# One norm for all tokens, the logits' products beside it, and a moved set of values in an attention layer's opening

## The chip, the cores and the metric

The kernel runs on one core of a Trainium2 chip. The metric is the device time of one launch in microseconds (us). Engines are named as in the profile: PE is TensorE's matmul row and PEld its weight loads, DVE is VectorE, ACT is ScalarE, POOL is GpSimd, SP is SyncE, which here issues DMAs. TensorE's clock has two levels in the records, 1.2 and 2.4 GHz, shown as a granted clock of 0.50 and 1.00.

## The reference, cut to what matters

Two layers over 1024 prompt tokens and 32 sample tokens (1056 columns in all, width 1024). Layer 0 is a gated convolution and a feed-forward block. Layer 1 is attention with a forget bias, then another feed-forward block.

```
kvf = rmsnorm(x, kv_norm) @ w_kv                 # keys, values, one forget logit per head
logf = log_sigmoid(kvf[..., 2 * D_ATT:] + b_f)
c = cumsum(concat(cached logf, logf))            # over tokens, per head
q = rmsnorm(x, b_norm) @ w_q
s = q @ k.T * HEAD_DIM ** -0.5 + c[query] - c[key]
o = softmax(where(key <= query, s, -inf)) @ v    # 16 heads of 64
x = x + o @ w_o
```

## The kernel before

Activations lie transposed: features on the 128 partitions, the 1056 tokens along the free axis. Weights and activations are split into a high and a low part, and each product of a 128x128 weight block is three matmuls (lines 259 to 261, `chain`). A unit of weights (128 output features) over all tokens is 72 such matmuls, in three chunks of tokens (384, 384 and 288 columns) of 8 steps.

A root-mean-square norm is one factor per token, and it is applied to the products rather than to x. `start` notes the sum of squares `acc`. The first units of a stage are multiplied out without it (`outer`), kept raw, and `settle` (line 296) then makes the factor and multiplies the raw tiles. `rstd` (line 313) makes it in three thirds of 352 tokens: `rstd_steps` (line 323) sums over partitions with one-column matmuls (line 334), takes a root on ScalarE (line 336), makes a Newton step on VectorE (lines 338 to 342), lays the factors on a diagonal `dg` (line 344), spreads them over all partitions with a matmul against ones (line 348) and copies them out (line 349). The mixer (layer 0) uses this for its first two units, the attention layer for its first.

The attention layer opens in `attention` (line 1259). `first` (line 1335) yields the values of the first pair of heads, then the keys and queries of head 0, step by step. `forget` (line 889) makes the logits and their running sums, and the two generators run in turns. `forget` multiplies the logits' weights by x (lines 913, 914), norms z (line 917), turns it (line 922), takes log-sigmoid on ScalarE and VectorE (lines 925 to 938), loads the cached logits into `frun` (line 943), sums over tokens with a triangle matmul (lines 950, 951), splits the sums into high and low parts (`ch`, `ekt`, `eqt`, lines 959 to 968), turns them (line 978), copies them out of PSUM (line 985) and writes them to DRAM (line 986). `rows` (line 1028) reads four rows per head back into partitions 64 to 67 of that head's operands `kb` and `qb`, which the second matmul of the scores uses (line 1092).

Then `weave` runs the attention of 16 heads as the main work and hangs filler steps between: `fillers(h)` (line 1326) gives head h the keys of head h + 1 (12 steps) and the values of the next pair (8 steps beside an even head, 4 beside an odd one). The last head's filler is the output product.

The order on each engine is not that of the code. The framework puts all instructions into queues before the run, by priority (earlier code first, raised by `high_priority` for attention's own work) and by its own estimates of time. On the chip each engine's queue is then in order. PSUM has six tiles in this phase: three named d, two s (two banks each) and one o. Of the 24 SBUF tiles of the pool "x", 16 hold the split activations here; the logits' tiles and the heads' operands share the others.

Of the kernel before, what the change touches and what calls it, by code (L numbers as in the profile page):

```python
# [18 lines left out]
D = 1024  # L19
SEQ = 1024  # L20
# [66 lines left out]
class Net:  # L87
# [187 lines left out]
    def unit(self, src, xs, dst, before=0):  # L275


        nc = self.nc
        h, l = self.ready.pop(0) if self.ready else self.weights(src)
        w = [(h[:, k], l[:, k]) for k in range(NK)]  # L280
        if self.fresh:
            for t, c in zip(self.outer(w, xs, CH), CH):
                for p, d in spread(c, before):
                    nc.scalar.activation(dst[:, d], t[:, p.start - c[0]:p.stop - c[0]], AF.Copy)
            self.raws.append((dst, before))
            self.fresh -= 1
            if not self.fresh:
                self.settle()
            return
        for c in CH:  # L290
            ps = self.dbank()[:, :c[1] - c[0]]
            self.chain(ps, w, xs, c)
            for p, d in spread(c, before):
                nc.vector.tensor_mul(dst[:, d], ps[:, p.start - c[0]:p.stop - c[0]], self.rs[:, p])

    def settle(self):

        for r, c in self.rstd(self.acc):
            for t, before in self.raws:
                for p, d in spread(c, before):  # L300
                    self.nc.vector.tensor_mul(t[:, d], t[:, d], r[:, p.start - c[0]:p.stop - c[0]])
# [8 lines left out]
        nc.scalar.activation(sq, x, AF.Square)  # L310
        return lambda: (nc.vector if hurry or m == NK - 1 else nc.gpsimd).tensor_add(acc, acc, sq)

    def rstd(self, acc, cuts=CH):

        out = self.rs = self.slot("rstd", None, F32, *self.rtag)
        for c in cuts:
            for _ in self.rstd_steps(acc, out, c):
                pass  # L320
            yield out[:, slice(*c)], c

    def rstd_steps(self, acc, out, c, own=False):

        nc = self.nc
        cs, n = slice(*c), (c[1] - c[0]) // SIDE

        def bank():
            return self.bank(self.spare()) if own else self.dbank()

        ps = bank()[:SIDE, :n]
        for i in range(n):
            a = c[0] + i * SIDE
            nc.tensor.matmul(ps[:, i:i + 1], acc[:, a:a + SIDE], self.ones[:, :1], start=True, stop=True)
        e, w, r = (self.sm.tile([SIDE, n], F32, name="n" + k, tag="n" + k, bufs=2) for k in "ewr")
        nc.scalar.activation(e, ps, AF.Sqrt, bias=self.epst[:SIDE], scale=1.0 / D)
        yield
        nc.vector.tensor_scalar(w, ps, -0.5 / D, -0.5 * EPS, op0=OP.mult, op1=OP.add)
        nc.vector.reciprocal(r, e)
        nc.vector.tensor_mul(e, r, r)  # L340
        nc.vector.tensor_mul(e, e, w)
        nc.vector.scalar_tensor_tensor(r, e, 1.5, r, op0=OP.add, op1=OP.mult)
        dg = self.diag([SIDE, n, SIDE])
        nc.vector.tensor_mul(dg, self.ident[:SIDE, None, :SIDE].to_broadcast([SIDE, n, SIDE]),
                             r[:, :, None].to_broadcast([SIDE, n, SIDE]))
        yield
        ps = bank()[:, :c[1] - c[0]]
        nc.tensor.matmul(ps, self.ones[:SIDE], dg.rearrange("p n c -> p (n c)"), start=True, stop=True)
        nc.scalar.activation(out[:, cs], ps, AF.Copy)
        yield  # L350
# [538 lines left out]
    def forget(self, xs):  # L889
# [14 lines left out]
        nc.vector.tensor_add(tri, tri, self.ident)  # L904
        f, u, v, d, e, lf, base, c = (self.keep("f" + n, [128, nb, H]) for n in "zuvdelbc")
        nc.vector.memset(f, 0.0)
        z = self.keep("z", [H, TT])
        low = self.keep("zl", [H, TT])
        for t in CH:
            n = t[1] - t[0]  # L910
            ps = self.bank("s")
            for k, (xh, xl) in enumerate(xs):
                nc.tensor.matmul(ps[:48, :n], w[:, k], xh[:, t[0]:t[1]], start=(k == 0), stop=False)
                nc.tensor.matmul(ps[:48, :n], w[:, k], xl[:, t[0]:t[1]], start=False, stop=(k == NK - 1))
            nc.scalar.activation(low[:, t[0]:t[1]], ps[32:32 + H, :n], AF.Copy)
            nc.vector.tensor_add(z[:, t[0]:t[1]], ps[:H, :n], low[:, t[0]:t[1]])
            nc.vector.tensor_mul(z[:, t[0]:t[1]], z[:, t[0]:t[1]], self.rs[:H, t[0]:t[1]])
        yield
        ps = self.bank("s")[:, :nb * H].rearrange("p (b h) -> p b h", h=H)
        for b in range(NK + 1):  # L920
# [17 lines left out]
        nc.vector.scalar_tensor_tensor(lf, f, 0.0, v, op0=OP.min, op1=OP.subtract)  # L938
        nc.sync.dma_start(a["o_f"][:SEQ].rearrange("(b p) h -> p b h", p=128), lf[:, :NK])
        nc.sync.dma_start(a["o_f"][SEQ:], lf[:ls, NK])  # L940
        run = self.keep("frun", [128, nb, H])
        nc.vector.memset(run, 0.0)
        nc.sync.dma_start(run[:, NK + 1], a["c_f"])
        nc.vector.tensor_copy(run[:, :NK], lf[:, :NK])
        nc.vector.tensor_copy(run[:ls, NK], lf[:ls, NK])
        for _ in range(3):
# [21 lines left out]
        nc.vector.tensor_sub(eq[:, :, :, 3], c, chf)  # L968
        yield
        yield  # L970
        for src, dst, old in ((ek, self.kb, self.cb), (eq, self.qb, None)):
            t = self.keep("er", [4 * H, TT])
            for b0 in range(0, NK + 1, 4):
                ps = self.bank("s")
                n = min(512, TT - b0 * 128)
                for b in range(b0, min(NK + 1, b0 + 4)):
                    m = min(128, TT - b * 128)
                    nc.tensor.transpose(ps[:4 * H, (b - b0) * 128:(b - b0) * 128 + m],
                                        src[:m, b].rearrange("p h r -> p (h r)"), self.ident[:m, :m])
                if b0 + 4 > NK and old is not None:  # L980
                    nc.tensor.transpose(ps[:4 * H, 128:256], src[:, NK + 1].rearrange("p h r -> p (h r)"), self.ident)
                    told = self.keep("er2", [4 * H, PAST])
                    nc.scalar.activation(told, ps[:4 * H, 128:256], AF.Copy)
                    nc.sync.dma_start(old, told)
                nc.scalar.activation(t[:, b0 * 128:b0 * 128 + n], ps[:4 * H, :n], AF.Copy)
            nc.sync.dma_start(dst, t)

    def scratch(self):

# [269 lines left out]
    def attention(self, x, parts, after):  # L1259
# [5 lines left out]
        self.heads, self.vs = [], {}  # L1265
        forget = self.forget(xs)

        def dense(src, gain, put):


            h, l = self.weights(src, gain)
            w = [(h[:, t], l[:, t]) for t in range(NK)]
            if self.fresh:
                raw = self.temp("raw")
                for t, c in zip(self.outer(w, xs, CA), CA):
                    nc.scalar.activation(raw[:, c[0]:c[1]], t, AF.Copy)
                self.raws.append((raw, 0))
                self.fresh = 0
                self.settle()
                for c in CA:  # L1280
                    put(raw[:, c[0]:c[1]], c)
                yield
                return
            for c in CA:
                d, n = self.dbank()[:, :c[1] - c[0]], c[1] - c[0]
                for k in range(NK):
                    self.chain(d, w, xs, c, range(k, k + 1))
                    if k % 2 and k + 1 < NK:
                        yield
                t = self.slot("stage", [128, 384], F32, "stage", 3)  # L1290
                nc.vector.tensor_mul(t[:, :n], d, self.rs[:, c[0]:c[1]])
                put(t[:, :n], c)
                yield

        def keys(h):
# [5 lines left out]
        def values(p):  # L1301
            vp = self.vs[p] = self.slot("vp", [128, NK + 1, 256], F32R, "vp", 2)
            yield from dense(a["w_v"][p], (self.gain[:, 2],), lambda t, c: self.values(p, vp, t, c))

        def outs():

# [19 lines left out]
        def fillers(h):  # L1326
            if h == HEADS - 1:
                return 3 * NK, outs()
            p = h // 2 + 1
            if p < NP and h % 2 == 0:  # L1330
                half[p] = values(p)
            n = (4 if h % 2 else 8) if p < NP else 0
            return 12 + n, mixed(h + 1, half.get(p), n)

        def first():
            yield from values(0)
            yield from keys(0)

        for _ in zip_longest(first(), forget):
            pass  # L1340
        self.rows(self.heads[0])
        self.weave(self.attend(), 13.0, fillers)
        self.wide = True
        ws = self.resident(a["w_o"][4:])
# [133 lines left out]
```

## Time and profile before

| what | value |
|---|---|
| median of 3 runs | 2549.89 us (2549.51 to 2549.95) |
| profiled execution | 2550.09 us |
| its span, first to last instruction | 2548.3 us |
| mean granted TensorE clock | 0.989 |
| PE busy | 2471.9 us, 97% of the span, 18484 matmuls |
| DVE, ACT, POOL busy | 1531.6, 1216.5 and 899.3 us |

The time of a launch is a little longer than the span of its instructions. A busy PE is not PE at its peak, since matmuls are pipelined and the clock can be granted at half; an idle engine other than the bounding one costs nothing. In a timeline row the brackets give how long the engine stood idle before it and what ended that wait.

### The profile page before, as it was taken

To read this page: it belongs to the slowest core of one execution; us is meant where nothing else is said; L and a number is where in the kernel's file an instruction comes from. 1 tells how busy PE (TensorE), PEld (TensorE's weight loads), DVE (VectorE), ACT (ScalarE), POOL (GpSimd) and SP (SyncE) were. 2 spreads that over 40 slices of the span, in tenths; PEclk is the share of its full clock that TensorE was granted. 3 is DMA by queue.
4 is the path that set the end of the run, shared out by engine and by line. 5 is a ranking of instruction groups with operands and counts; after the bars stand their busy time and mean duration, and the time that the engine had idled before them with its cause. 6 is when DMAs were issued, how large, how long until landed. Compare 5 with 4: busy or idle time off the path is not lost. (4 is left out here: it accounts for less than half of the span.)

```text
span 2548.3 us, 47227 instructions
## 1 busy us (share of the span) xinstructions
PE 2471.9 (97%) x18484; PEld 2433.1 (95%) x18484; DVE 1531.6 (60%) x2617; ACT 1216.5 (48%) x2388; POOL 899.3 (35%) x952
## 2 busy tenths in 40 slices
PE   7999999999999999998999999999999999999996
PEld 6999999999999999997999999999999999999996
DVE  5434438855555555665677677665875555555575
ACT  4111114555555555444566666653454555555454
POOL 3000012344444444342455444422244444443423
PEclk9999999999999999998999999999999999999998
DMA  3111123376766666631233222373247676666752
GB/s 111 45 48 50 42 77 98 70 120 120 122 119 114 116 118 119 139 113 50 75 80 80 77 76 71 80 251 104 72 88 125 116 121 119 111 117 116 122 141 69
DMA packets 147631, 254.76 MB, mean 100 GB/s; under 512 B 22352, under 2 KB 58320, under 8 KB 147408
## 3 DMA queue, kind: packets, MB, share of 16 engines
q0 software_dynamic: 41472, 77.88, 23.0%
q1 hardware_dynamic: 105936, 173.87, 22.7%
q8 instruction: 145, 2.38, 0.4%
q14 instruction: 78, 0.64, 0.1%
HBM read 130.52 MB, written 113.04 MB: 96 GB/s over the span
## 5 line engine op out<-in xcount | busy, mean ns | idle before, releaser
L711 PE MATMUL pb_p<-b,wb 128*128 128x264 f32 x6720 | 894.9, 284 | 1.8 <-ACT u L753 1.8
L711 PEld LDWEIGHTS pb_p<-b,wb 128*128 128x128 f32 x6720 | 850.0, 188 | 2.2 <-ACT u L753 2.2
L877 POOL DMA_DIRECT2D xd<-xs x288 | 262.1, 914 | 494.9 <-ACT xs L875 493.6
L875 ACT ACTIVATE xs<-pb_d 128x264 f32<-128x264 f32 x576 | 218.3, 387 | 349.4 <-PE pb_d L261 309.8
L259 PE MATMUL pb_d<-acth,wb 128*128 128x264 f32 x1152 | 327.8, 285 | 1.6 <-ACT xs L875 1.6
L260 PE MATMUL pb_d<-actl,wb 128*128 128x264 f32 x1152 | 327.5, 285 | 0.0
L261 PE MATMUL pb_d<-acth,wb 128*128 128x264 f32 x1152 | 327.3, 285 | 0.0
L259 PE MATMUL pb_d<-xh,wh 128*128 128x384 f32 (+2 forms) x864 | 285.3, 333 | 8.4 <-ACT xh L248 7.6
L260 PE MATMUL pb_d<-xl,wh 128*128 128x384 f32 (+2 forms) x864 | 285.2, 330 | 5.6 <-DVE xl L249 5.5
L261 PE MATMUL pb_d<-xh,wl 128*128 128x384 f32 (+2 forms) x864 | 283.6, 328 | 0.0
L478 DVE SCALAR_TENSOR_TENSOR y<-u,cv,y 128x1058 f32<-128x1058 f32 x186 | 238.8, 1329 | 54.9 <-ACT y L474 54.8
L259 PEld LDWEIGHTS pb_d<-acth,wb 128*128 128x128 f32 x1152 | 216.6, 188 | 2.8 <-ACT xs L875 2.5
L261 PEld LDWEIGHTS pb_d<-acth,wb 128*128 128x128 f32 x1152 | 216.8, 188 | 0.0
L260 PEld LDWEIGHTS pb_d<-actl,wb 128*128 128x128 f32 x1152 | 216.8, 188 | 0.0
L236 ACT ACTIVATE wh<-wraw 128x1024 fp32r<-128x1024 f32 (+1 forms) x69 | 72.3, 1047 | 259.6 <-PE pb_o L260 125.3
L460 POOL COPY u<-cv 128x4 f32<-128x4 f32 x96 | 63.5, 662 | 355.7 <-DVE u L668 256.9
L701 DVE TENSOR_TENSOR wb<-wr,wb 128x512 fp32r<-128x512 f32 x196 | 154.2, 788 | 56.0 <-ACT wb L700 44.7
L701 DVE TENSOR_TENSOR wb<-ws,wb 128x512 fp32r<-128x512 f32 x160 | 126.1, 789 | 98.6 <-ACT wb L700 98.6
L259 PEld LDWEIGHTS pb_d<-xh,wh 128*128 128x128 f32 x864 | 164.7, 191 | 9.8 <-ACT xh L248 8.0
L260 PEld LDWEIGHTS pb_d<-xl,wh 128*128 128x128 f32 x864 | 165.1, 191 | 7.9 <-DVE xl L249 7.4
L733 POOL TENSOR_TENSOR ws<-wr 128x512 f32<-128x512 f32 x80 | 121.7, 1521 | 134.9 <-DMA wr<-in_w_up 120.8
L261 PEld LDWEIGHTS pb_d<-xh,wl 128*128 128x128 f32 x864 | 164.8, 191 | 0.3
(347 smaller groups left out, 4964.2 us busy)
## 6 DMA issues: line engine op xcount, KB each, us to landing
xd<-xs POOLq DMA_DIRECT2D x288, 264.0 KB, 4.3
wr<-in_w_up SPq DMA_DIRECT2D x168, 256.0 KB
wr<-in_w_down SPq DMA_DIRECT2D x80, 256.0 KB
x<-xd SPq DMA_DIRECT2D x48, 264.0 KB
wraw<-in_w_in SPq DMA_DIRECT2D x23, 512.0 KB
xd<-x SPq DMA_DIRECT2D x64, 132.0 KB
wraw<-in_w_kq SPq DMA_DIRECT2D x16, 512.0 KB
xd<-x SPq DMA_DIRECT2D x16, 264.0 KB
```

The source lines that it names most:

```text
L236: nc.scalar.activation(h[:, i:j], raw[:, i:j], AF.Copy)
L259: nc.tensor.matmul(ps, wh, xh[:, c[0]:c[1]], start=(i == 0), stop=False)
L260: nc.tensor.matmul(ps, wh, xl[:, c[0]:c[1]], start=False, stop=False)
L261: nc.tensor.matmul(ps, wl, xh[:, c[0]:c[1]], start=False, stop=(i == n - 1))
L460: self.nc.gpsimd.tensor_copy(v, st.rearrange("p (a b) -> p a b", b=2))
L478: self.nc.vector.scalar_tensor_tensor(y, u[:, i:i + TC], w[:, i:i + 1], y, op0=OP.mult, op1=OP.add)
L701: nc.vector.tensor_sub(t[:, 1], src, t[:, 0].bitcast(F32))
L711: nc.tensor.matmul(ps[:, q, :QB], w[:, i, k], t[:, j, cs], start=(begin and k == 0 and n == 0), stop=(end and k == len(b) - 1 and n == 2), ...
L733: getattr(self.nc.gpsimd, "tensor_" + op)(dst, x, y)
L875: nc.scalar.activation(t[:, q * QB:(q + 1) * QB], ps, AF.Copy)
L877: nc.gpsimd.dma_start(d, t, accum_op=OP.add)
```

## The change

It makes the norm's factor once for all 1056 tokens at the opening of the mixer and of attention, in a generator that stops after the diagonal. `forget` runs its products at that stop and multiplies z in one instruction afterwards. `frun` and its load of cached logits move to the start of `forget`. The transposes of the bias rows become `turned`, under a raised priority, with one copy per 1024 columns, the queries' half on VectorE. In `first`, the first pair's transposes move behind the first chunk of head 0's keys, and the 12 steps of the second pair's values run there instead of beside heads 0 and 1; each chunk of these values is put away two steps into the next chunk. Cut to its core (calls of `settle` in the mixer run it through, and `newton` and `means` hold lines 333 to 345 of before):

```diff
@@ settle, rstd
-        for r, c in self.rstd(self.acc):
+        steps = self.rstd(self.acc)
+        next(steps)
+        yield
+        for r, c in steps:
             for t, before in self.raws:
...
-    def rstd(self, acc, cuts=CH):
+    def rstd(self, acc):
         out = self.rs = self.slot("rstd", None, F32, *self.rtag)
-        for c in cuts:
-            for _ in self.rstd_steps(acc, out, c):
-                pass
+        n = TT // SIDE
+        room = self.temp("nrm")[:SIDE, :3 * n].rearrange("p (i n) -> p i n", n=n)
+        e, w, r = (room[:, i] for i in range(3))
+        ps = self.bank(self.spare())[:SIDE, :n]
+        self.means(ps, acc, 0, e)
+        dg = self.newton(ps, e, w, r)
+        yield
+        for c in CH:
+            a, b = c[0] // SIDE, c[1] // SIDE
+            ps = self.dbank()[:, :c[1] - c[0]]
+            self.nc.tensor.matmul(ps, self.ones[:SIDE], dg[:, a:b].rearrange("p n c -> p (n c)"), start=True, stop=True)
+            self.nc.scalar.activation(out[:, slice(*c)], ps, AF.Copy)
             yield out[:, slice(*c)], c
@@ forget
         nc.vector.memset(f, 0.0)
+        run = self.keep("frun", [128, nb, H])
+        nc.vector.memset(run, 0.0)
+        nc.sync.dma_start(run[:, NK + 1], a["c_f"])
...
             nc.vector.tensor_add(z[:, t[0]:t[1]], ps[:H, :n], low[:, t[0]:t[1]])
-            nc.vector.tensor_mul(z[:, t[0]:t[1]], z[:, t[0]:t[1]], self.rs[:H, t[0]:t[1]])
+        yield
+        nc.vector.tensor_mul(z, z, self.rs[:H])
         yield
...
-        run = self.keep("frun", [128, nb, H])
-        nc.vector.memset(run, 0.0)
-        nc.sync.dma_start(run[:, NK + 1], a["c_f"])
...
+        with self.tc.high_priority(offset=3 * AHEAD):
+            self.turned(ek, eq)
+        self.rows(self.heads[0])
+
+    def turned(self, ek, eq):
+        nc = self.nc
+        for src, dst, copy in ((ek, self.kb, lambda o, i: nc.scalar.activation(o, i, AF.Copy)),
+                               (eq, self.qb, nc.vector.tensor_copy)):
+            t = self.keep("er", [4 * HEADS, TT])
+            ps, rest = self.bank("s")[:4 * HEADS], self.bank("o")[:4 * HEADS]
+            for b in range(NK + 1):
+                m = min(128, TT - b * 128)
+                out = ps[:, b * 128:(b + 1) * 128] if b < NK else rest[:, :m]
+                nc.tensor.transpose(out, src[:m, b].rearrange("p h r -> p (h r)"), self.ident[:m, :m])
...
+            copy(t[:, :SEQ], ps)
+            copy(t[:, SEQ:], rest[:, :TT - SEQ])
             nc.sync.dma_start(dst, t)
...
@@ attention
-        def dense(src, gain, put):
-            h, l = self.weights(src, gain)
+        def dense(src, gain, put, early=None):
+            h, l = early or self.weights(src, gain)
...
-                self.settle()
+                steps = self.settle()
+                next(steps)
+                yield
+                for _ in steps:
+                    pass
+                yield
                 for c in CA:
                     put(raw[:, c[0]:c[1]], c)
...
                     self.chain(d, w, xs, c, range(k, k + 1))
+                    if early and k == 1 and c != CA[0]:
+                        put(*last)
...
-                put(t[:, :n], c)
+                last = t[:, :n], c
+                if not early or c == CA[-1]:
+                    put(*last)
...
-            if p < NP and h % 2 == 0:
+            if 1 < p < NP and h % 2 == 0:
                 half[p] = values(p)
             n = (4 if h % 2 else 8) if p < NP else 0
+            if p == 1:
+                n = 0
...
         def first():
-            yield from values(0)
-            yield from keys(0)
+            mine, others = values(0), keys(0)
+            for _ in range(2):
+                next(mine)
+                yield
+            for _ in range(4):
+                next(others)
+                yield
+            next(mine)
+            half[1] = values(1, self.weights(a["w_v"][1], (self.gain[:, 2],)))
+            yield
+            yield from others
+            for _ in range(12):
+                next(half[1])
+                yield
```

## Rows read from the trace of the kernel before

**Rows 1.** The head of the profile's page.

```profile
span 2548.3 us, 47227 instructions
```

**Rows 2.** Windows, attention's opening: length, then PE, PEld, DVE, ACT, POOL, PEclk, DMA share, GB/s.

```profile
1136.00:1147.70 11.70, 11.64 (x72) 11.67 (x73) 8.21 (x12) 2.67 (x6) 5.55 (x5) 1.00 0.25 76
1147.70:1156.00 8.30, 8.30 (x59) 6.53 (x58) 2.26 (x8) 4.03 (x7) 3.24 (x2) 1.00 0.22 64
1156.00:1170.20 14.20, 10.75 (x48) 8.30 (x48) 8.00 (x26) 5.35 (x12) 1.03 (x1) 0.64 0.11 40
1170.20:1185.30 15.10, 15.10 (x94) 14.93 (x93) 11.70 (x32) 9.96 (x20) 2.94 (x3) 1.00 0.16 32
1185.30:1204.30 19.00, 10.91 (x45) 9.04 (x45) 6.88 (x20) 7.80 (x18) 5.91 (x8) 0.73 0.32 78
1204.30:1242.00 37.70, 36.99 (x252) 35.71 (x252) 22.55 (x57) 19.82 (x44) 11.65 (x10) 1.00 0.20 55
```

**Rows 3.** TensorE's timeline, the norm: start us, us, what [idle before, its releaser].

```profile
1150.45 0.71 PE L334 MATMUL pb_d<-ones,acc 128*88 128x1 f32 x8
...
1158.38 0.26 PE L922 MATMUL pb_s<-ident,z 16*128 16x16 f32 x2 [1.07 <-DVE nr L339]
1159.57 1.19 PE L348 MATMUL pb_d<-dg,ones 88*128 88x352 f32 x2 [0.94 <-DVE dg L344]
...
1162.31 0.50 PE L922 MATMUL pb_s<-ident,z 16*128 16x16 f32 x3 [0.51 <-DVE z L917]
1163.69 1.51 PE L348 MATMUL pb_d<-dg,ones 88*128 88x352 f32 x2 [0.88 <-DVE dg L344]
...
1167.81 0.69 PE L259 MATMUL pb_d<-xh,wh 128*128 128x384 f32 x1
```

**Rows 4.** TensorE's timeline, from the running sums to the first scores.

```profile
1179.49 0.43 PE L950 MATMUL pb_s<-frun,tri 128*128 128x160 f32 x2
...
1187.30 1.04 PE L978 MATMUL pb_s<-ident,ekt 128*64 128x128 f32 x8 [1.85 <-DVE ekt L966]
...
1190.97 0.49 PE L1091 MATMUL pb_s<-ka,qa 128*128 128x128 f32 x2 [0.27 <-ACT er L985]
1196.69 0.79 PE L1092 MATMUL pb_s<-kb,qb 68*128 68x128 f32 x2 [5.22 <-DMA qb<-qbd]
```

**Rows 5.** VectorE's timeline of the same stretch.

```profile
1153.40 0.52 DVE L344 TENSOR_TENSOR dg<-ident,nr 88x352 f32<-88x352 f32 x1
...
1166.17 0.51 DVE L917 TENSOR_TENSOR z<-z,rstd 16x352 f32<-16x352 f32 x1
...
1182.71 2.36 DVE L1019 TENSOR_TENSOR ka<-stage,ka 64x288 fp32r<-64x288 f32 x1
1185.10 0.45 DVE L1020 TENSOR_TENSOR qa<-stage,qa 64x288 fp32r<-64x288 f32 x1
```

**Rows 6.** SyncE's timeline: when two DMAs were issued.

```profile
1177.01 0.42 SPq L943 DMA_DIRECT2D frun<-in_c_f  x1
...
1194.60 0.25 SPq L1031 DMA_DIRECT2D qb<-qbd  x1
```

**Rows 7.** Busy time by window, the mixer's opening.

```profile
41.40:46.40 5.00, 0.75 (x11) 0.69 (x9) 2.46 (x7) 3.31 (x6) 0.00 (x0) 0.74 0.16 39
46.40:54.00 7.60, 7.60 (x28) 7.04 (x29) 2.11 (x8) 0.72 (x2) 0.00 (x0) 0.50 0.12 50
```

**Rows 8.** Busy time by window, three later heads: 16, 20 and 12 filler steps.

```profile
1372.90:1406.00 33.10, 31.94 (x218) 30.33 (x217) 25.54 (x58) 23.38 (x55) 19.06 (x17) 1.00 0.33 84
1406.00:1438.90 32.90, 32.90 (x231) 32.12 (x230) 20.74 (x46) 17.57 (x39) 12.91 (x11) 1.00 0.27 70
1671.50:1702.20 30.70, 29.50 (x208) 28.19 (x207) 22.38 (x57) 17.44 (x38) 7.28 (x6) 1.00 0.85 288
```

**Rows 9.** VectorE's timeline, head 0's largest block: first mask and last scaling.

```profile
1210.13 1.08 DVE L1072 CUSTOM_DVE_ANT_0 prob<-pb_s,mask 128x896 f32<-128x896 f32 x1
...
1214.47 1.35 DVE L1079 TENSOR_SCALAR prob<-prob,st 128x896 f32<-128x896 f32 x2
```

More of the change, by code (lines that the diff above doesn't have):

```diff
@@ L287, in unit @@
             if not self.fresh:
-                self.settle()
+                for _ in self.settle():
+                    pass
             return
@@ L331, in rstd_steps, with means, newton @@
         ps = bank()[:SIDE, :n]
-        for i in range(n):
-            a = c[0] + i * SIDE
-            nc.tensor.matmul(ps[:, i:i + 1], acc[:, a:a + SIDE], self.ones[:, :1], start=True, stop=True)
         e, w, r = (self.sm.tile([SIDE, n], F32, name="n" + k, tag="n" + k, bufs=2) for k in "ewr")
-        nc.scalar.activation(e, ps, AF.Sqrt, bias=self.epst[:SIDE], scale=1.0 / D)
+        self.means(ps, acc, c[0], e)
         yield
+        dg = self.newton(ps, e, w, r)
+        yield
+        ps = bank()[:, :c[1] - c[0]]
+        nc.tensor.matmul(ps, self.ones[:SIDE], dg.rearrange("p n c -> p (n c)"), start=True, stop=True)
+        nc.scalar.activation(out[:, cs], ps, AF.Copy)
+        yield
+    def means(self, ps, acc, at, e):
+        for i in range(ps.shape[-1]):
+            a = at + i * SIDE
+            self.nc.tensor.matmul(ps[:, i:i + 1], acc[:, a:a + SIDE], self.ones[:, :1], start=True, stop=True)
+        self.nc.scalar.activation(e, ps, AF.Sqrt, bias=self.epst[:SIDE], scale=1.0 / D)
+    def newton(self, ps, e, w, r):
+        nc, n = self.nc, ps.shape[-1]
         nc.vector.tensor_scalar(w, ps, -0.5 / D, -0.5 * EPS, op0=OP.mult, op1=OP.add)
@@ L345, in rstd_steps @@
                              r[:, :, None].to_broadcast([SIDE, n, SIDE]))
[L346 to L350, printed above, removed]
+        return dg
     def diag(self, shape):
@@ L970, in forget @@
         yield
[L971 to L985, printed above, removed]
+        with self.tc.high_priority(offset=3 * AHEAD):
[11 more added lines that the diff above has]
+                nc.tensor.transpose(out, src[:m, b].rearrange("p h r -> p (h r)"), self.ident[:m, :m])
+            if src is ek:
+                nc.tensor.transpose(rest[:, 128:256], src[:, NK + 1].rearrange("p h r -> p (h r)"), self.ident)
+            copy(t[:, :SEQ], ps)
+            copy(t[:, SEQ:], rest[:, :TT - SEQ])
             nc.sync.dma_start(dst, t)
+            if src is ek:
+                told = self.keep("er2", [4 * HEADS, PAST])
+                copy(told, rest[:, 128:256])
+                nc.sync.dma_start(self.cb, told)
     def scratch(self):
@@ L1278, in dense @@
                 self.fresh = 0
-                self.settle()
+                steps = self.settle()
+                next(steps)
+                yield
+                for _ in steps:
+                    pass
+                yield
                 for c in CA:
@@ L1299, in keys, with values @@
             yield from dense(a["w_kq"][h], (self.kq[:, 0], self.kq[:, 1]), lambda t, c: self.fill(s, t, c))
-        def values(p):
+        def values(p, early=None):
             vp = self.vs[p] = self.slot("vp", [128, NK + 1, 256], F32R, "vp", 2)
-            yield from dense(a["w_v"][p], (self.gain[:, 2],), lambda t, c: self.values(p, vp, t, c))
+            yield from dense(a["w_v"][p], (self.gain[:, 2],), lambda t, c: self.values(p, vp, t, c),
+                             early)
         def outs():
@@ L1329, in fillers @@
             p = h // 2 + 1
-            if p < NP and h % 2 == 0:
+            if 1 < p < NP and h % 2 == 0:
                 half[p] = values(p)
             n = (4 if h % 2 else 8) if p < NP else 0
+            if p == 1:
+                n = 0
             return 12 + n, mixed(h + 1, half.get(p), n)
         def first():
-            yield from values(0)
-            yield from keys(0)
+            mine, others = values(0), keys(0)
[7 more added lines that the diff above has]
+            half[1] = values(1, self.weights(a["w_v"][1], (self.gain[:, 2],)))
+            yield
+            yield from others
+            for _ in range(12):
+                next(half[1])
+                yield
         for _ in zip_longest(first(), forget):
             pass
-        self.rows(self.heads[0])
         self.weave(self.attend(), 13.0, fillers)
```

## The prediction

> **What bounds the kernel now.** I read the page first: the span is 2548.3 us [rows 1]. The profiled execution took 2550.09 us, 1.8 us more than its span and 0.2 us more than the median of the three runs, 2549.89; the sum is made against 2550.1. TensorE is busy nearly all the way, so I looked for the stages where it is not, with busy times by window, and the opening of attention stands out [rows 2]. There 72 matmuls of one weight unit take 11.64 of 11.70 us at the full clock (granted 1.00, 2.4 GHz): no loss. The logits' products, up to 1156, also run without a gap. Then come two losses, with a full stretch between them (94 matmuls in 15.10 us).
>
> Loss A, 1156.0 to 1170.2: busy 10.75 of 14.2 us, mean granted clock 0.64. The timeline of TensorE says why [rows 3]: four pauses, 1.07, 0.94, 0.51 and 0.88 us, each before a step of the norm or the logits, released by VectorE. The norm is made in three thirds, one behind the other, and the first product of head 0's keys starts only at 1167.81. The mean of 0.64 is 10.2 us at 0.50 (1.2 GHz); some 8.4 us of that were busy, and half of busy time at half the clock is lost: 4.2 us. With 3.45 us idle, A is 7.65 us.
>
> Loss B, 1185.3 to 1204.3: busy 10.91 of 19.0 us, clock 0.73. The timeline shows a pause of 1.85 us for the bias rows' VectorE work and one of 5.22 us until the rows are back from DRAM (released by the transfer qb<-qbd) [rows 4]. Idle 8.1 us; from 1196.7 to 1204.3 the engine is busy at half clock, 3.8 us lost. B is 11.9 us, A and B together 19.5 us. That is what the change can win here.
>
> **The chain behind B.** The scores wait for rows that come from z: z is normed by 1166.7, goes through softplus to the running sum, waits for the cached logits (transfer issued at 1177.01, the matmul that needs it at 1179.49), and is transposed, written to DRAM and read back (last read issued 1194.60) [rows 4 to 6].
>
> **The change, part by part.**
> One norm. Sums, root, Newton steps and diagonal are made once over 12 columns in place of three times over 4. From the first third's sums (1150.45) to its diagonal's end (1153.40 + 0.52) the chain takes 3.5 us [rows 3, 5]. The wide one adds two more groups of sums (0.6 us each, from 0.71 with overlap) and two more widths of diagonal (0.45 each): 5.6 us. It no longer needs one of the three banks that the first unit fills, so it can begin at 1147.7 and be done near 1153.5, while the logits' products run: they last to 1147.7 + 7.6 (their window's 8.3 less 0.7 of sums) + 1.9 (all sums) = 1157.2 [rows 2, 3]. The three broadcast matmuls (0.6 each at full clock, from 1.51 and 1.19 at half) end at 1159, and head 0's keys start there, not at 1167.8. So the pauses of A go. The cover is the products; were they short, the pauses would be 2 us, not 3.45.
> z. The copy of the last third and one z multiply (three widths of 0.51) put z at about 1161, 5.7 us earlier than 1166.7 [rows 5]. The cached logits are loaded ahead, which removes the 2.5 us between its issue and the matmul. So the bias rows land at 1196.7 - 8.2 = 1188.5. The turned transposes with fewer, wider copies (the queries' half on VectorE) save or cost little: bounds 1 us won and 0.5 lost, since no row has such a copy on VectorE; I take none. Raising their priority costs nothing while other matmuls stand behind.
> The second pair's values. Their 72 matmuls (11.64 us) and their 8 block transposes (8 such took 1.04 us [rows 4]) stand ahead of the first scores; nothing is added, since heads 0 and 1 lose them. From 1159 TensorE has keys 0 (11.6), these values (11.6), both pairs' transposes (2.1) and the logits' own small matmuls (an estimate from their rows, about 4): to about 1188.5. The rows land then too, so the 5.22 us wait is covered, with nothing to spare, and the half clock behind it goes.
> What is queued behind. Values 1 use the weight slots that the first unit frees at 1147.7, and no operand slots of the keys; keys 1 get theirs once keys 0 are done, 15 us before their first use. On SP the values' three stores and the next weights now stand ahead of the rows' transfers; they are issues of about 0.5 us, inside the same slack. The late put of a chunk (behind the next chunk's second step) keeps TensorE off its own eviction; it is worth under 1 us per chunk.
> What is late next. The order of queues is fixed before the run by estimates, so TensorE can stand behind a step that comes late. A gap costs its length, and one long enough to lose the clock as in A costs about 4 more. Bounds for what stays of A and B: 0 and 8.9 (B's wait and its half clock). I take 3.7: a couple of short pauses (about 2 us) and something under half of a 4 us fall of the clock, nearer to the low end since the rows put cover next to every wait.
> Heads 0 and 1. They keep 12 filler steps each, where they had 20 and 16. A head of 16 steps idles 1.16 us (33.1 less 31.94), one of 20 none, and the late head that has 12 and a part of the next stage idles 1.2 [rows 8]. Of the two opening heads the first idles 0.7 now [rows 2], and I take as much for the second. I charge 1.8 us for both; bounds 0 and 11.6 (that they do not shrink at all).
> The mixer's opening uses the same norm. Now TensorE idles 4.25 us there (5.00 less 0.75) and then runs 7.6 us at 0.50 [rows 7]. The new sums must wait for the bank of the last eviction, the root's table load hides them, the diagonal ends 0.9 us later, and all broadcasts then come at once. If the third unit's products are put ahead of it, up to 2.5 us come back; if not, 0.9 is lost. I take 0.
> Sum: 19.5 - 3.7 - 1.8 + 0 = 14.0 us, so 2536.
>
> VectorE's operand split took 2.36 us at 1182.71, and the next one of the same width 0.45 [rows 5]. The row is what one collision in this chain costs, 1.9 us, and it stays in my sum. The Trainium skill (SBUF — State Buffer, Who interferes with whom) says a VectorE instruction with two SBUF inputs is fully held by a GpSimd instruction that reads SBUF. By that, each of the three GpSimd passes over the next head's weights could fall on the earlier chain and hold it, 3.8 us more than the one in the sum: 2540.
>
> **The rivals.**
> The rows come late. The bias chain shares VectorE, ScalarE and the operand buffers with keys 0 and the values, and its transposes stand in TensorE's one queue. If they are placed behind the values, the round trip is waited out after them: 5.2 idle and 3.8 of half clock stay, 19.5 - 9.0 - 1.7 (the rest of what stays) - 1.8 = 7 won, 2543. For it: the two ends meet with no slack. Against it: the raised priority. Chance 0.17.
> The heads give it back. If heads 0 and 1 are set by the softmax chain, the moved matmuls shorten them little; with 9 of 11.6 us not gained, 14 - 9 + 1.8 = 7 would be 2543, all of it 2546. Against it: the 12-step head above. Chance 0.09.
> No effect. If keys 0 cannot get operand buffers while the logits' tiles hold them (one of these is now held from the start), the same waits move a few microseconds along: 2548 to 2550. Chance 0.06.
> Slower. Place: heads 0 and 1. A block's softmax, from first mask to last scaling, takes 5.7 us for the largest (1210.13 to 1214.47 + 1.35) [rows 9], so up to 22.8 us per head of four blocks. With fewer filler matmuls, what keys do not cover is idle time. It decides from 14 us in the two heads, 7 us each, a third of that bound; at 10 each the kernel takes 2536 + 20 = 2556. Against it: 1.2 us idle in the 12-step head. Chance 0.04.
>
> **How the numbers follow.** My forecast has 0.64: 2536, own range 2530 (nothing stays of A and B, mixer gains) to 2541. About 0.2%, 5.1 us, is what a measurement of this kernel tells from no change, so faster means under 2544.8. The late rows are nearly all faster (0.15 of 0.17), the heads' case in part (0.05 of 0.09): faster 0.84. Same: 0.02 + 0.04 + 0.05 = 0.11. Slower: 0.04, and 0.01 of no effect, 0.05. The range takes in both 2543 cases: 2529.5 to 2545.5.
>
> **What would show it.** Right: one group of sums, one root and one diagonal in the opening; head 0's keys at about 1159; no wait for qb<-qbd of over 1 us; granted clock 1.00 from there to the first heads; the first scores near 1189 with all of values 1 done; head 0 shorter by 6 us or more. Wrong: a pause of several microseconds before the first bias product, a clock at 0.50 anywhere from 1148 to 1205, heads 0 and 1 as long as now.

## The result and the profile after

The changed kernel takes 2530.49 us (median of 4 runs, 2527.23 to 2532.86) where the kernel before took 2549.7 in the same session: a ratio of 0.9923, 95% interval 0.9909 to 0.9936, 19.2 us less. Forecast were 2536 and a range of 2529.5 to 2545.5. The profiled execution took 2527.23 us, 22.9 less than the 2550.09 of before.

The head of the page, beside [rows 1]:

```profile
span 2525.4 us, 47206 instructions
...
PE 2462.6 (98%) x18484; PEld 2425.1 (96%) x18484; DVE 1525.6 (60%) x2593; ACT 1213.8 (48%) x2380; POOL 898.5 (36%) x952
```

Both kernels have 18484 matmuls, nearly in one order, so the two traces can be laid side by side: the table gives the start of the n-th matmul after, less its start before, worked out from the records of both profiled executions.

```
matmul number   401    1801   2401   8251   9201   12001  18401
start before    89.4   313.9  403.2  1140.7 1303.1 1721.7 2521.0
after - before  -7.9   -7.9   -9.5   -10.1  -23.4  -23.5  -22.7
```

The gain comes in two places: 7.9 us in the mixer's opening, which my sum had at nothing, and 13.3 us in attention's (from 10.1 to 23.4), which it had at 14.0. Some 2 us more lie elsewhere, and they are not the change's: a second profiled execution of the changed kernel (2530.69 us) has 7.9 us and 12.8 us in the same two places, and 1.3 us lost elsewhere where this one has 1.7 gained. The stretches in which the granted clock was 0.50, from the records (start, and length in us):

```
before  43.8 (10.24)  368.1 (3.41)  1095.1 (3.41)  1160.0 (10.24)  1194.1 (10.24)  2480.9 (3.41)  2535.5 (14.80)
after   353.8 (3.41)  1186.7 (6.83)  2456.4 (3.41)  2473.5 (3.41)  2511.1 (16.41)
```

The mixer's opening by windows, the stretches of [rows 7], columns as in [rows 2]:

```profile
41.40:46.40 5.00, 5.00 (x41) 5.00 (x39) 1.23 (x1) 3.12 (x5) 0.00 (x0) 1.00 0.15 44
46.40:54.00 7.60, 7.60 (x52) 7.28 (x52) 2.05 (x6) 0.42 (x2) 0.00 (x0) 1.00 0.12 47
```

TensorE's timeline there:

```profile
45.23 1.97 PE L359 MATMUL pb_o<-ones,acc 128*88 128x1 f32 x24
...
53.05 1.94 PE L332 MATMUL pb_d<-dg,ones 88*128 88x352 f32 x6
```

Before, the engine was busy 0.75 of 5.00 us and then ran at 0.50. Now it has no pause and 1.00 throughout: the sums are one group of 24 matmuls, the broadcasts one group of six, 7.8 us later, and the third unit's matmuls stand in front, between and behind.

Attention's opening by windows:

```profile
1137.60:1149.00 11.40, 11.40 (x81) 8.92 (x80) 5.51 (x11) 5.46 (x10) 4.71 (x3) 1.00 0.18 55
1149.00:1162.30 13.30, 13.30 (x91) 13.03 (x91) 7.74 (x19) 5.74 (x10) 0.00 (x0) 1.00 0.13 43
1162.30:1175.00 12.70, 12.50 (x80) 11.76 (x79) 10.60 (x29) 7.40 (x15) 3.61 (x3) 1.00 0.28 78
1175.00:1187.00 12.00, 11.01 (x66) 9.44 (x64) 4.94 (x13) 6.79 (x16) 7.27 (x7) 0.99 0.62 157
1187.00:1196.00 9.00, 7.59 (x34) 6.48 (x35) 6.50 (x19) 5.61 (x15) 2.61 (x3) 0.64 0.02 7
1196.00:1218.00 22.00, 21.72 (x154) 20.93 (x153) 15.25 (x38) 14.68 (x33) 10.29 (x9) 1.00 0.29 75
1218.00:1252.70 34.70, 33.41 (x225) 31.57 (x224) 23.32 (x58) 22.71 (x53) 16.63 (x18) 1.00 0.27 66
```

From 1137.6 to 1175 the engine idles 0.2 us at the full clock, where [rows 2] had 3.45 us of pauses and a clock of 0.64: loss A is gone. What stays lies between 1175 and 1196, in the first blocks of head 0. TensorE's timeline, norm to first blocks:

```profile
1137.68 1.97 PE L359 MATMUL pb_o<-ones,acc 128*88 128x1 f32 x24
...
1144.66 1.94 PE L332 MATMUL pb_d<-dg,ones 88*128 88x352 f32 x6
...
1148.98 0.34 PE L259 MATMUL pb_d<-xh,wh 128*128 128x384 f32 x1
...
1153.93 0.69 PE L949 MATMUL pb_s<-ident,z 16*128 16x16 f32 x9
...
1164.95 0.43 PE L974 MATMUL pb_s<-frun,tri 128*128 128x160 f32 x2
...
1173.36 1.04 PE L1009 MATMUL pb_s<-ident,ekt 128*64 128x128 f32 x8 [0.20 <-DVE ekt L990]
...
1178.80 0.42 PE L259 MATMUL pb_d<-xh,wh 128*128 128x384 f32 x1
...
1183.45 0.50 PE L1124 MATMUL pb_s<-kb,qb 68*128 68x128 f32 x2 [0.20 <-DMA qb<-qbd]
...
1188.41 0.79 PE L1123 MATMUL pb_s<-ka,qa 128*128 128x512 f32 x1 [1.78 <-DVE st L1104]
```

The wait for the bias rows is 0.20 us in place of 5.22 [rows 4]. The row at 1178.80 is the first chunk of head 1's keys, 24 matmuls, which the planner (the framework's ordering of the queues before the run) put ahead of the first bias product; nothing in my sum had it there. Behind, 1.78 us go by waiting for VectorE's softmax, in the half-clock stretch that begins at 1186.7.

The bias chain on VectorE, as [rows 5]:

```profile
1150.21 1.25 DVE L944 TENSOR_TENSOR z<-z,rstd 16x1056 f32<-16x1056 f32 x1
...
1163.24 0.15 DVE L969 COPY frun<-fl 32x16 f32<-32x16 f32 x1
...
1167.35 2.43 DVE L1051 TENSOR_TENSOR ka<-stage,ka 64x288 fp32r<-64x288 f32 x1 [0.55 <-ACT ka L1048]
...
1172.79 0.42 DVE L990 TENSOR_TENSOR ekt<-ch,fc 128x160 f32<-128x160 f32 x1
...
1173.20 0.45 DVE L992 TENSOR_TENSOR eqt<-fc,ch 128x160 f32<-128x160 f32 x1
```

### The profile page after: what moved, and what is told of

It reads as the page before. It is cut to its first block, busy times and chain, and to the rows that moved or that the text cites. A ratio compares the mean times of both kernels' runs of the same rounds, so it can differ in the third digit from the quotient of the medians.

```text
span 2525.4 us, 47206 instructions
## 1 busy us (share of the span) xinstructions
PE 2462.6 (98%) x18484; PEld 2425.1 (96%) x18484; DVE 1525.6 (60%) x2593; ACT 1213.8 (48%) x2380; POOL 898.5 (36%) x952
## 3 DMA queue, kind: packets, MB, share of 16 engines
q1 hardware_dynamic: 105936, 173.87, 22.9%
```

## The experiments

Twelve runs, in three sessions, each beside the kernel before. "In attention" below is the shift between matmuls 8251 and 9201 against the profiled execution of before, worked out as in the table above (13.3 us for the whole change). It leaves out what the clock does elsewhere. It has an error of about 2 us: in the run with the mixer alone, whose attention is that of before, it reads 2.1 (1.0 us less idle, and 1.1 less lost by half clock).

**The mixer alone.** The kernel before, with one wide norm in the mixer and thirds in attention.

```diff
...
 def rstd(self, acc, cuts=CH):
+    if self.temps[0] == "slot":
+        yield from self.rstd_wide(acc)
+        return
```

> The kernel before with the one wide norm in the mixer's opening alone; attention opens as before. Theory (the term that I put at 0 was mis-sized: the wide norm leaves the next banks free, so the third unit's matmuls fill the 4.25 us pause and the half-clock stretch behind it does not come): 7 to 10 us faster than before, about 2540 to 2543, with no TensorE pause over 1 us and a granted clock of 1.00 between 40 and 60 us. Rival (the mixer's part is worth what I predicted, -0.9 to 2.5 us): 2547 to 2551.

Measured: 2539.89 us, ratio 0.9962 (0.9947 to 0.9976), 9.9 less. Matmul 401 starts 7.9 us sooner, as in the whole change, and no half clock is left between 40 and 60 us. The other 2 us lie in attention, whose code this run leaves alone. The 7.9 us are the piece that my sum missed.

**The mixer, thirds kept, with another bank.** Sums and broadcasts use bank o, not the rotation of the units' products.

```diff
-            for _ in self.rstd_steps(acc, out, c):
+            for _ in self.rstd_steps(acc, out, c, self.temps[0] == "slot"):
```

> The kernel before with the norm still in three thirds, but in the mixer its sums and broadcasts use the bank named o and not the next three of the rotation. Theory banks (what held the third unit back was the bank it would get, not the length of the norm): the third unit's matmuls follow the second unit at once, and nearly all of the 7 to 10 us comes, 2540 to 2543. Rival (the single wide norm itself is what pays): three thirds still come one behind the other and TensorE waits for them, 2546 to 2550.

Measured: 2546.87 us, 0.999 (0.998 to 0.9999), 2.9 less. TensorE's timeline:

```profile
45.34 0.71 PE L334 MATMUL pb_o<-ones,acc 128*88 128x1 f32 x8
...
65.97 1.03 PE L348 MATMUL pb_o<-dg,ones 88*128 88x352 f32 x2 [1.85 <-DVE dg L344]
67.55 0.66 PE L259 MATMUL pb_o<-xh,wh 128*128 128x352 f32 x1 [0.55 <-ACT rstd L349]
```

The 4.25 us pause of the first third is gone: the third unit's products follow at once, so it was the rotation's bank that had kept them behind the norm. But the thirds, one behind the other in bank o and dealt out among the products, now last until 66 us. At the last of them TensorE waits again: the next products are in bank o too and stand behind the norm's copy. Half clock for 6.83 us goes with it. The bank alone moves the wait; the single pass, whose sums sit in bank o as well, removes it. A single pass with its sums in the rotation's bank was not run.

**Attention alone.** The changed kernel with the mixer's norm in thirds again.

```diff
 def rstd(self, acc):
+    if self.temps[0] == "slot":
+        yield
+        for c in CH:
+            for _ in self.rstd_steps(acc, out, c):
+                pass
+            yield out[:, slice(*c)], c
+        return
```

> The changed kernel with the old norm in three thirds in the mixer; attention opens as changed. Theory (parts add up): the mixer's 8 us are lost again and attention's 12 to 15 stay, 2535 to 2538, with the 4.25 us pause back at 42 us. Rival (the mixer's part matters little and attention holds all of the 19 us): 2529 to 2533.

Measured: 2538.58 us, 0.9956 (0.9941 to 0.9971), 11.2 less, 12.3 in attention. With the mixer's 9.9 that is 21.1, against 19.2 for both: the two add, within the scatter of the runs.

**The values left beside the heads.** The changed kernel, with the second pair's values where they were.

```diff
-            if 1 < p < NP and h % 2 == 0:
+            if p < NP and h % 2 == 0:
                 half[p] = values(p)
-            if p == 1:
-                n = 0
...
-            half[1] = values(1, self.weights(a["w_v"][1], (self.gain[:, 2],)))
-            for _ in range(12):
-                next(half[1])
-                yield
```

> The changed kernel with the second pair's values left beside heads 0 and 1, as before the change; norm, early cached logits and turned rows as changed. Theory (the values are the cover of the rows' round trip): the rows land near 1183, keys 0 end near 1163 and only keys 1 can stand in, so a pause of 4 to 8 us and a half-clock stretch return; 5 to 9 us slower than the changed kernel, 2535 to 2540. Rival (earlier rows and the norm are the whole gain, keys 1 cover as well as values 1, and the ramp of heads 0 and 1 is better with more filler): within 2 us of the changed kernel or faster, 2526 to 2533.

Measured: 2538.51 us, 0.9956 (0.9942 to 0.9971), 8.0 above the whole change and 1.4 below the mixer alone. TensorE's timeline:

```profile
1175.01 1.89 PE L1009 MATMUL pb_s<-ident,ekt 128*64 128x128 f32 x8 [6.28 <-DVE ekt L990]
...
1180.21 0.38 PE L1123 MATMUL pb_s<-ka,qa 128*128 128x256 f32 x1 [1.10 <-DVE er L1012]
...
1185.19 0.80 PE L1124 MATMUL pb_s<-kb,qb 68*128 68x128 f32 x2 [4.60 <-DMA qb<-qbd]
```

The norm's pauses are gone here too, yet 12.0 us are waited out behind it, where before it was 7.1 (1.85 and 5.22 [rows 4]). What the norm saves, the bias chain takes back as soon as nothing covers it: the chain sets when the scores may start, and matmuls done sooner only wait longer.

**Eight steps of values ahead, four beside head 0.**

```diff
-                n = 0
+                n = 0 if h else 4
...
-            for _ in range(12):
+            for _ in range(8):
```

> The whole change, with only 8 of the second pair's 12 steps of values ahead of the first scores and the last 4 beside head 0. In the whole change the first scores with the bias rows start 0.20 us after the cover ends, so the cover has no slack. Theory (all twelve steps are needed as cover): the 24 matmuls taken away are 3.2 us at full clock, the wait for the rows grows by up to that and the clock may drop behind it; the ramp of head 0 gets those 3.2 us back and loses its pause of 1.78 us. Sum 0 to 4 us slower than the whole change, 2530 to 2535. Rival (eight steps are cover enough, and the ramp is what lacks work): the pause of 1.78 us and part of the 6.83 us at half clock go, 2525 to 2528.

Measured: 2536.17 us, 0.9941 (0.9924 to 0.9957), 5.7 above the whole change: more than either theory gave. TensorE's and ScalarE's timelines:

```profile
1188.87 0.80 PE L1124 MATMUL pb_s<-kb,qb 68*128 68x128 f32 x2 [8.58 <-DMA qb<-qbd]
...
1177.59 0.42 ACT L1089 ACTIVATE cache<-craw 64x256 fp32r<-64x256 f32 x1 [3.22 <-DMA craw<-in_c_k]
...
1178.42 1.00 ACT L1002 ACTIVATE er<-pb_s 64x1024 f32<-64x1024 f32 x1
```

The wait is 8.58 us, where the missing cover is 3.2. The rest is not cover: the rows themselves came later. In this run ScalarE has the conversion of the cached keys ahead of the copies of the bias rows and waits 3.22 us for their load; the queries' rows were written 8.8 us after `eqt` was ready (1175.15 to 1183.95), in the whole change 4.9 (1173.65 to 1178.56). So the run mixes less cover with a changed order, and does not show how many steps are needed.

**Head 1's keys sooner.** The changed kernel, with the pace of head 0's fillers begun 3 of 13 units ahead.

```diff
-                head, at, n = h, 0.0, 0
+                head, at, n = h, 0.0 if h else 3.0, 0
```

> The whole change, with head 0's filler steps (head 1's keys) brought forward by 3 of the head's 13 units of weight, so that about three more steps stand in the ramp of head 0's scores. Theory (the ramp, 1183 to 1196, loses 1.78 us of pause and 3.4 us by the half clock because no filler stands there): 2 to 5 us faster than the whole change, 2525.5 to 2528.5, and no half clock between 1183 and 1196. Rival (the later blocks of head 0 then lack those steps and pause instead): within 1 us of the whole change, 2529.5 to 2531.5, with pauses for VectorE's softmax near 1205 to 1218.

Measured: 2525.13 us, 0.9906 (0.9891 to 0.992), 15.3 in attention. Windows of that run:

```profile
1175.00:1187.00 12.00, 11.97 (x79) 11.62 (x77) 4.13 (x11) 6.74 (x16) 7.30 (x7) 1.00 0.60 159
1187.00:1196.00 9.00, 8.28 (x45) 6.23 (x43) 8.04 (x22) 6.62 (x16) 4.54 (x5) 1.00 0.17 40
```

The idle time from 1175 to 1196 falls from 2.40 to 0.75 us, and the clock stays at 1.00.

**The values alone.** The kernel before, with only the values moved (their chunks put away late, as in the change, and head 0's rows read at once).

```diff
...
         def first():
             yield from values(0)
+            half[1] = values(1, self.weights(a["w_v"][1], (self.gain[:, 2],)))
             yield from keys(0)
+            for _ in range(12):
+                next(half[1])
+                yield
...
-            n = (4 if h % 2 else 8) if p < NP else 0
+            n = (4 if h % 2 else 8) if 1 < p < NP else 0
```

> The kernel before, with only the second pair's values moved ahead of the first scores (and head 0's rows read as soon as they are written); norms in thirds, logits, transposes and load of cached logits as before. Theory (the values are the cover for the rows' round trip, whatever the norm does): the 5.22 us wait goes, and with it most of the half clock behind it; loss A stays. As much as the same move is worth on top of the norm, 8.0 us: 2541 to 2543. Rival (cover and norm need each other: without the earlier z the rows land at 1196.7 and more, after the cover's end near 1194): a wait of 2 to 3 us and a half-clock stretch stay, 2544 to 2547.

Measured: 2547.01 us, 0.9991 (0.9981 to 1.0), hardly to be told from no change. TensorE's timeline:

```profile
1193.18 1.04 PE L978 MATMUL pb_s<-ident,ekt 128*64 128x128 f32 x8
...
1197.52 0.60 PE L978 MATMUL pb_s<-ident,eqt 128*64 128x128 f32 x4
...
1198.55 0.74 PE L978 MATMUL pb_s<-ident,eqt 128*64 128x128 f32 x5
...
1207.50 0.47 PE L1093 MATMUL pb_s<-kb,qb 68*128 68x128 f32 x2 [3.25 <-DMA qb<-qbd]
```

The theory fell. The rival's time came nearly true, but its rows were later than it had them: the first bias product stood at 1207.50, 10.8 us later than before (1196.69 [rows 4]), though `ekt` and `eqt` were ready (1190.6) only 2.8 us later. The old transposes were dealt out among the values' matmuls, so the cover delayed what it was to cover.

**The old transposes.** The changed kernel without `turned` and its priority.

```diff
-        with self.tc.high_priority(offset=3 * AHEAD):
-            self.turned(ek, eq)
+        for src, dst, old in ((ek, self.kb, self.cb), (eq, self.qb, None)):
...
         self.rows(self.heads[0])
```

> The whole change, with the transposes of the bias rows as before (three narrower copies per half, all on ScalarE, no raised priority). My sum took this part at nothing, with bounds of 1 us won and 0.5 us lost. Theory: 2530.5, within 1.5 us of the whole change. Rival (the raised priority is what brings the rows in time, since the transposes would otherwise stand behind more of the values' matmuls): the rows land 2 to 4 us later, the first bias product waits that long for the transfer, and the time is 2533 to 2537.

Measured: 2534.83 us, 0.9939 (0.9924 to 0.9953), 4.3 above the whole change, 6.5 in attention where that has 13.3. TensorE's timeline:

```profile
1181.06 0.74 PE L1002 MATMUL pb_s<-ident,eqt 128*64 128x128 f32 x5
...
1188.40 0.77 PE L1117 MATMUL pb_s<-kb,qb 68*128 68x128 f32 x2 [5.56 <-DMA qb<-qbd]
```

From the end of ekt's and eqt's work on VectorE (1173.36) to the bias product it is 15.0 us; in the whole change 9.8 (1173.65 to 1183.45). The last transposes of `eqt` come 7.7 us after it is ready. The rival's time stood. What I had at nothing is worth 4 to 7 us once values stand beside it. The run takes away the raised priority and the wide copies together, so it does not show which of the two brings this; the rival named only the priority.

**Values and new transposes, norm in thirds.** On top of the kernel with the values alone:

```diff
...
+        with self.tc.high_priority(offset=3 * AHEAD):
+            self.turned(ek, eq)
...
```

> The kernel before, with the second pair's values moved ahead of the first scores and the bias rows' transposes of the change (one wide copy per half, raised priority); norms in thirds and the late load of the cached logits as before. With the values alone, ekt and eqt were ready at 1190.6 but the first bias product waited until 1207.50 (3.25 us of it with nothing else to do), 16.9 us later; in the whole change the same way took 9.8 us (1173.65 to 1183.45). Theory (the values push the old transposes back, and the raised priority is the condition for the move): the rows arrive near 1200.5, before the cover ends near 1204, so the wait of 3.25 us and most of the half clock behind it go: 5 to 7 us faster than the values alone, 2540 to 2542; what is then left to the whole attention part (e3, 2538.6) is 2 to 4 us for the wide norm. Rival (the lateness is SyncE's queue or the chain itself, not the transposes): within 1.5 us of the values alone, 2545.5 to 2548.5.

Measured: 2547.6 us, 0.9989 (0.998 to 0.9998), no faster than the values alone. TensorE's timeline:

```profile
1201.31 0.39 PE L1100 MATMUL pb_s<-kb,qb 68*128 68x128 f32 x2
...
1206.63 0.80 PE L1099 MATMUL pb_s<-ka,qa 128*128 128x512 f32 x1 [1.84 <-DVE st L1080]
...
1247.39 0.58 PE L1099 MATMUL pb_s<-ka,qa 128*128 128x256 f32 x1 [1.11 <-DVE st L1080]
```

Half of the theory held: no wait for qb<-qbd is left, and the first bias product stands at 1201.31, 6.2 us sooner. Half of that is the transposes' (it is 13.8 us behind `eqt` in place of 16.9); in this execution `eqt` itself was ready 3.1 us sooner. Its time did not hold. Stretches at half clock begin at 1158.3 (13.65 us, in the norm), 1206.1 and 1247.0 (6.83 us each), the last two at these waits of heads 0 and 1. From matmul 8251 to 9201 TensorE idles 7.5 us, with the values alone 8.9, but loses 12.4 us by half clock (half of its busy time there) in place of 9.1. So in that execution the clock took back what the wait gave; the executions with no profile can't be read this way.

**Sooner still.** As head 1's keys sooner, with 5.0 for 3.0.

> The whole change with head 0's filler steps brought forward by 5 of 13 units in place of 3. Theory (the ramp was short by one or two pauses, which 3 units have filled): nothing more to win, and the late blocks of head 0 begin to pause: 2525 to 2528. Rival (more cover, more gain): 2522.5 to 2524.5, fewer waits for VectorE between 1185 and 1200.

Measured: 2533.74 us, 0.9935 (0.9921 to 0.9948): 3.0 above the whole change of the same session, where single runs of the two overlap, and outside of both forecasts. TensorE's and ScalarE's timelines:

```profile
1193.16 0.61 PE L1160 MATMUL pb_d<-ident,prob 128*128 128x128 f32 x3 [2.42 <-DVE prob L1111]
1194.54 0.60 PE L1123 MATMUL pb_s<-ka,qa 128*128 128x384 f32 x1 [0.77 <-DVE st L1104]
...
1188.85 0.42 ACT L1089 ACTIVATE cache<-craw 64x256 fp32r<-64x256 f32 x1 [2.20 <-DMA craw<-in_c_k]
...
1189.80 1.28 ACT L1107 ACT_TABLE_LOAD   x1
```

The first bias product came about as soon after `eqt` as with 3 units (12.0 us, there 11.7). What came late is the softmax: ScalarE has the conversion of the cached keys ahead of it and waits 2.20 us for their load, as in the run with eight steps ahead. TensorE then waits for the softmax, and half clock for 6.83 us follows at 1194.7. So this run is slower by an order that changed beside the edit, and says little on more cover.

**Both versions once more, in one session.**

> The whole change once more, beside the kernel with head 1's keys sooner, for a comparison in one session. Theory: 2530.5 median, and the runs lie 2527 to 2533 apart by which of the short half-clock stretches (3.41 us near 354, 1087, 2456 and 2473) a run has.

> The whole change with head 0's filler steps 3 units sooner, once more. Theory (the ramp's pause and half clock are gone, about 1.8 + 3.4 us): 4 to 5.5 us under the whole change of the same session. Rival (the first measurement had fewer of the stretches at half clock by chance): under 2.5 us.

Measured: the whole change 2530.73 us (2527.3 to 2533.21), ratio 0.9922 (0.9908 to 0.9935); with the keys sooner 2528.37 (2524.61 to 2529.98), 0.9911 (0.9898 to 0.9925). In attention they read 12.8 and 15.3. So the keys are worth 2 to 2.5 us by the two pairs of traces and 2.4 and 5.4 by the medians; the intervals of the ratios overlap, and the 4 to 5.5 that I gave are not borne out: side by side the rival's "under 2.5 us" stood. The best version found is this one, by a margin that these runs do not settle.

## Why the prediction was right, and where it was not

**The time** was right to 5.5 us and inside the range, but only 1.0 us above its lower end: of the eight executions of the changed kernel three (2527.23, 2527.3 and 2528.8) lie below it. The parts were not all right. Worked against the profiled execution: mixer 7.9 (I had 0), attention 13.3 (I had 14.0), about 1.7 elsewhere. The mixer's miss alone is larger than what the range left on that side of the forecast; and attention came out by errors that cancel, which is luck.

**The mixer's opening: the mis-sized term.** I wrote "up to 2.5 us come back; if not, 0.9 is lost. I take 0". The run with it alone is 9.9 us faster, and 7.9 of them are at this place. The products of the third unit did go ahead of the norm, which I had named as the good end, but the price was wrong: [rows 7] shows 4.25 us idle and 7.6 us at half clock, of which 3.8 are lost. Together that is 8.05, and the trace gained 7.9. I counted A and B in just this way and not the same pattern at 41 us. The bound of 2.5 came from no row. The run with bank o shows what I did not see: the first pause was a matter of which bank the norm sat in, and with thirds it comes back at 66 us.

**Loss A, 7.65 us, goes.** One group of sums, of roots and of diagonals, head 0's keys at 1148.98: with the 10.1 us that this stage starts sooner, 1159.1, where I wrote 1159. (By the records 8.8 us of A's half-clock stretch were busy, not 8.4, so A was nearer to 7.8.)

**The bias rows, by two errors that cancel.** z was ready at 1151.46, in the time of before 1161.6, nearly as I had it (1161). I then had the rows at 1188.5; the first bias product stood at 1183.45 + 10.1 = 1193.5, 5 us later. Where they went: z's transposes stood in TensorE's queue until 1153.93, behind the first chunk of head 0's keys, so that VectorE's next step came 3.2 us after z where it had been 1.2. The early load of the cached logits gave 1.8 us and not 2.5: from the last copy into `frun` to its first matmul it was 3.37 us before (VectorE's row of before below, and 1179.49 [rows 4]) and is 1.56 now (1163.39 to 1164.95), behind the values in TensorE's queue. And from that matmul to the first bias product it is 18.5 us, before 17.2. These three make 4 of the 5 us.

```profile
1175.97 0.15 DVE L945 COPY frun<-fl 32x16 f32<-32x16 f32 x1
```

That the wait is 0.20 us all the same is due to the first chunk of head 1's keys (1178.80), cover that I had not counted. The rest of the cover ends at 1178.80 + 10.1 = 1188.9, where I had 1188.5. Without that chunk the late rows would have been waited for, as in my rival.

**`turned`: at nothing in my sum, and the condition for the rest.** "Raising their priority costs nothing" is beside the point. Without the priority and the wide copies the rows come about 5 us later and 4.3 us of the gain are lost; the rival of the late rows (2543) is in kind what the run with the old transposes shows (2534.83).

**The parts need each other.** Against before, the norm with `turned` and no moved values reads 3.3 us in attention, values alone 2.8, values with `turned` 0.8, the norm with the values and the old transposes 6.5, with an error of about 2; all three together read 13.3. ("The norm" has the early load of the cached logits with it; no run takes these two apart.) My sum took A and B as two terms to be added. They are one chain: whatever ends sooner ahead of it only lengthens the next wait, until early rows and cover are there at once.

**What stays of A and B.** I took 3.7 us. The trace has 2.40 us idle from 1175 to 1196, and 6.83 us at half clock, of which some 5 busy: 2.5 lost. That makes 4.9, at the waits for softmax in head 0. It is also a sign that I had named as wrong: a clock of 0.50 between 1148 and 1205 (1186.7 + 10.1 = 1196.8 in the time of before). It is less than before and not gone. The heads, at 1.8 (a charge between my bounds that no row gives as it stands), idle 0.28 and 1.29 us in the last two windows. From the first bias product to matmul 9201 it is 106.4 us before and 96.3 after, half clock included, where 11.6 us of matmuls went out. So neither the rival that they give it back nor the slower one showed.

**VectorE and GpSimd.** VectorE's split with both inputs in SBUF took 2.43 us at 1167.35, and GpSimd's pass began 0.29 us before it and ended 0.32 us before its end. GpSimd's and VectorE's timelines:

```profile
1167.06 2.40 POOL L237 TENSOR_TENSOR wl<-wraw,wh 128x1024 fp32r<-128x1024 f32 x1 [19.58 <-ACT wh L236]
...
1179.04 2.40 POOL L237 TENSOR_TENSOR wl<-wraw,wh 128x1024 fp32r<-128x1024 f32 x1 [1.40 <-PE pb_d L1077]
...
1146.54 1.33 DVE L305 TENSOR_TENSOR raw<-raw,rstd 128x352 f32<-128x352 f32 x1
```

The Trainium skill (SBUF — State Buffer, Who interferes with whom) has a VectorE instruction with two SBUF inputs contend with a GpSimd instruction that reads SBUF, by an exclusive lock, and this row agrees. So does a second one: a multiply of the raw values took 1.33 us at 1146.54, under a GpSimd pass of 1146.16 to 1147.48, where one of before took 0.52; z did not wait for it. The pass at 1179.04 met no such instruction of the chain. So one collision was paid in the chain and not three: the sum from the row held, and the 2540 by the rule did not come.

## What to carry to other kernels

A pause and the half clock behind it are to be priced together: read both off for every stage that the change touches, the ones it was not made for too. Moved work covers a wait only if the steps that end the wait are kept ahead of it in every queue; test both together, since each alone may be worth next to nothing. Where queues are ordered by a planner, an edit of one step can change the order of others: look for a new wait on every engine before a slower run is put down to the edit. And once a chain, not an engine, sets the start of a stage, time saved ahead of it is no gain until something fills the wait.

## What was not expected of the hardware

The same program does not lose the clock at the same places: a stretch of 3.41 us at half clock near 1086 stood in the second profiled execution of the changed kernel (2530.69 us) and not in the first (2527.23), which has one near 2473 instead. The runs of one kernel lie some 6 us apart, as much as several of the differences measured here. The clock is only a part of that: of these two executions the slower idles 1.8 us more and loses 0.4 us more by half clock, out of 3.5. Behind the same old norm in the mixer, half clock lasted 10.24 us in the profile of before and 6.83 in three other runs (attention alone, values alone, values and new transposes). Pauses of 1.1 us for VectorE in head 1 were followed by half clock in two kernels (3.41 us at 1236.6 with eight steps ahead, 6.83 at 1247.0 with values and new transposes) and by none in the whole change (1.11 us at 1228.47). Why is left open.
